# The scheduler's highest rank for the recurrence of a gated DeltaNet layer

## The chip, the cores and the metric

The kernel runs on one core of a Trainium2 chip. The metric is the device time of one execution in microseconds. The core has five engines that work side by side, each through its own queue and in the order of that queue: TensorE (PE in the profile, its weight loads PEld), VectorE (DVE), ScalarE (ACT), GpSimd (POOL) and SyncE (SP), which issues the DMA transfers here.

## The reference

A trunk of two residual layers over 1024 tokens of width 1024, with a last normalization. The even layer has dilated window attention and an HGRN2 recurrence; the change does not touch it. The odd layer is a gated DeltaNet with 8 key heads and 16 value heads of width 128. Its core, cut down:

```python
def odd_mixer(hn, w_in, conv_w, dt_bias, a_log, norm_w, w_out):
    qkv, z, b_logit, a_logit = _split(hn @ w_in, ODD_SIZES)
    qkv = silu(causal_depthwise_conv(qkv, conv_w))
    q, k, v = _split(qkv, (C_KEY_WIDTH, C_KEY_WIDTH, C_VAL_WIDTH))
    ...
    o = gated_delta_rule_chunked(q, k, v, g, beta)
    o = rms_norm(o, norm_w) * silu(z)
    return o @ w_out

def gated_delta_rule_chunked(q, k, v, g, beta):
    # S_t = exp(g_t)(I - b_t k_t k_t^T) S_{t-1} + b_t k_t v_t^T ; o_t = S_t^T q_t
    ...
    sol = triangular_solve(a_mat, rhs, lower=True, unit_diagonal=True)
    u, w = sol[..., :dv], sol[..., dv:]
    def step(state, inp):
        u_n, w_n, a_n, qd_n, kt_n, gl_n = inp
        v_new = u_n - w_n @ state
        o = qd_n @ state + a_n @ v_new
        new_state = state * gl_n + kt_n.T @ v_new
        return new_state, o
```

Every chunk needs the state that the chunk before it left: the step is a chain.

## The kernel before

The 1024 tokens stand as 8 tiles of 128 (NT = 8), and the recurrence goes in 8 chunks of 128 tokens. The odd layer goes through 8 heads `hh`, each one key head with its two value heads (`e` = 0, 1). For each head there are three kinds of work:

- `proj(j)`: the projections by `proj_cols`, in which each product is three matmuls of 128x512 (high and low parts, `mm3`, L143 to L145), for key (pk), two values (pv) and query (pq), each followed by a convolution in `conv` (L822 to L831) on ACT and DVE. `conv` holds a tile `ub`, of which there is one; the projections have two PSUM banks ("pj"). The first thing in `proj(j)` is `way_out(j - 2)`: the normalization of an earlier head's output (POOL, L928), its gate projection (oz), its transposes (ot, L935) and its gating (oy, L937). Weights come by SP (raww) and are split by ACT (w_hi, L112) and DVE (w_lo, L113), one unit ahead of use.
- `invert(hh)`: the inverse of the triangular matrix: products kk (L986), decays gcl (L977, L978), L (L992), copies Lg (L999), then 62 DVE operations, each needing the one before (tm and Tp, L1007 and L1009), then small matmuls (qp, up, q, u).
- `recur(hh)`: the chain. Chunk c: ks = kT·S (L1105); r = ks scaled, plus v (L1108, DVE, two); qs = q·S (L1111); oq = qs scaled (L1114, ACT, two); vp = U·r (L1120); vt = vp scaled (L1123, DVE); vn = copy of vp (L1125, ACT); kv = kn·vt (L1129); S new = S scaled plus kv (L1133, DVE, two); op = A·vn (L1140); then `attend(c + 1)`, which asks for the decays of the chunk after (`decay_a`: a gca load on SP, an addition on POOL at L1079, two exponentials on ACT at L1081) and makes the next chunk's A (qk, L1091, on PE; A, L1093, on DVE); bv = op plus oq (L1143, DVE); oj, squares with their sum (L1148, ACT, two). qs, vp and qk share one PSUM bank ("d"); ks, kv and op share two ("b"); gca and A have two tiles, S two, and r, oq, vt and vn one each.

Three `yield`s cut a chunk into steps. The last loop of the layer emits them mixed with the next head's work: after each step of `recur(hh)`, `mix` emits 2.8 units of `blend(invert(hh + 1), proj(hh + 1))`. For the last head this is the way out of head 6, the gate of head 7 and the first output projections.

What the engines then do is settled when the program is built. A scheduler goes through time by its own model of durations, and on each engine, among the instructions whose inputs and tiles are there, takes the one of lowest rank. An instruction's rank is its place in emission. So in the odd layer the order on every engine, TensorE among them, comes from emission order and the scheduler's model; nothing there is ordered by hand. (The attention of the even layer is emitted in a region that orders TensorE by hand.) On the chip each engine keeps that order and waits on semaphores.

Of the kernel before, what the change touches and what calls it, by code (L numbers as in the profile page):

```python
# [18 lines left out]
P = 128  # L19
D = 1024  # L20
T = 1024
NT = T // P
# [56 lines left out]
def trunk_kernel(ctx: ExitStack, tc: tile.TileContext, x, ew, ewo, ow, owab, owo, nw, fnw, lbl, hnw,  # L79
                 cw, dtb, alog, onw, cst, out):  # L80
    nc = tc.nc
    dve, act, pe, pool = nc.vector, nc.scalar, nc.tensor, nc.gpsimd
# [8 lines left out]
    def bank(tag, shape, name):  # L91
        return pp.tile(shape, F32, name=name, tag=tag, bufs=BANKS[tag])
# [647 lines left out]
    def odd_layer(es):  # L740
        sp = es.enter_context(tc.tile_pool(name="od", bufs=1))
        gt = {n: sp.tile([P, NT, 16], F32, name=f"g_{n}") for n in ("beta", "gc", "ngc", "eg", "nbeg", "etl", "egl")}
# [70 lines left out]
        KT, KN, SC, Q, BV, CQ, SS, VT, US = {}, {}, {}, {}, {}, {}, {}, {}, {}  # L813
# [258 lines left out]
        def recur(hh):  # L1072

            kT, kn, q, bv, U = KT[hh], KN[hh], Q[hh], BV[hh], US[hh]
            ss = SS[hh] = sp.tile([P, NT, 2], F32, name=f"oss{hh}", tag="oss", bufs=2)

            def decay_a(c):
                DA = decays(hh, c, "a")
                pool.tensor_tensor(DA, DA, MA[:, None, :].to_broadcast([P, 2, 128]), op=ALU.add)  # L1079
                for e in range(2):  # L1080
                    act.activation(DA[:, e, :], DA[:, e, :], AF.Exp, bias=gt["ngc"][:, c, 2 * hh + e:2 * hh + e + 1])  # L1081
                return DA

            def attend(c):

                DA = ahead_a.pop()
                if c < NT - 1:
                    ahead_a.append(decay_a(c + 1))
                qk = bank("d", [P, 128], f"qk{hh}_{c}")
                s = slice(c * 128, (c + 1) * 128)  # L1090
                pe.matmul(qk, kT[:, s], q[:, s], start=True, stop=True)  # L1091
                A = sp.tile([P, 2, 128], F32, name=f"A{hh}_{c}", tag="A", bufs=2)
                dve.tensor_tensor(A, qk[:, None, :].to_broadcast([P, 2, 128]), DA, op=ALU.mult)  # L1093
                return A

            ahead_a = [decay_a(0)]
            yield 1.0
            A = attend(0)
            St = None
            for c in range(NT):  # L1100
                col = [slice(2 * hh + e, 2 * hh + e + 1) for e in range(2)]
                s = slice(c * 128, (c + 1) * 128)
                if c:
                    ks = bank("b", [P, 2, 128], f"ks{hh}_{c}")
                    pe.matmul(ks, kT[:, s], St, start=True, stop=True)  # L1105
                    r_ = sp.tile([P, 2, 128], F32, name=f"r{hh}_{c}", tag="r")
                    for e in range(2):
                        dve.scalar_tensor_tensor(r_[:, e, :], ks[:, e, :], SC[hh][:, 1, c, e:e + 1],  # L1108
                                                 bv[:, c, e, :], op0=ALU.mult, op1=ALU.add)
                    qs = bank("d", [P, 2, 128], f"qs{hh}_{c}")  # L1110
                    pe.matmul(qs, q[:, s], St, start=True, stop=True)  # L1111
                    oq = sp.tile([P, 2, 128], F32, name=f"oq{hh}_{c}", tag="oq")
                    for e in range(2):
                        act.activation(oq[:, e, :], qs[:, e, :], AF.Copy, scale=gt["eg"][:, c, col[e]])  # L1114
                else:
                    r_ = bv[:, 0]
                yield 1.0
                vp = bank("d", [P, 2, 128], f"vp{hh}_{c}")
                for e in range(2):
                    pe.matmul(vp[:, e, :], U[:, 2 * c + e, :], r_[:, e, :], start=True, stop=True)  # L1120
                if c < NT - 1:
                    vt = sp.tile([P, 2, 128], F32, name=f"vt{hh}_{c}", tag="vt")
                    dve.tensor_tensor(vt, vp, gt["etl"][:, c, 2 * hh:2 * hh + 2, None].to_broadcast([P, 2, 128]), op=ALU.mult)  # L1123
                vn = sp.tile([P, 2, 128], F32, name=f"vn{hh}_{c}", tag="vn")
                act.copy(vn, vp)  # L1125
                yield 1.0
                if c < NT - 1:
                    kv = bank("b", [P, 2, 128], f"kv{hh}_{c}")
                    pe.matmul(kv, kn[:, c, :], vt, start=True, stop=True)  # L1129
                    Sn = sp.tile([P, 2, 128], F32, name=f"S{hh}_{c}", tag="S", bufs=2)  # L1130
                    if c:
                        for e in range(2):
                            dve.scalar_tensor_tensor(Sn[:, e, :], St[:, e, :], gt["egl"][:, c, col[e]],  # L1133
                                                     kv[:, e, :], op0=ALU.mult, op1=ALU.add)
                    else:
                        dve.tensor_copy(Sn, kv)
                    St = Sn
                op = bank("b", [P, 2, 128], f"op{hh}_{c}")
                for e in range(2):
                    pe.matmul(op[:, e, :], A[:, e, :], vn[:, e, :], start=True, stop=True)  # L1140
                A = attend(c + 1) if c < NT - 1 else None
                if c:
                    dve.tensor_tensor(bv[:, c], op, oq, op=ALU.add)  # L1143
                else:
                    dve.tensor_copy(bv[:, c], op)
                for e in range(2):
                    jk = sp.tile([P, 128], BF16, name=f"oj{hh}_{c}_{e}", tag="jk", bufs=2)
                    act.activation(jk, bv[:, c, e, :], AF.Square, accum_out=ss[:, c, e:e + 1])  # L1148
                yield 1.0


# [41 lines left out]
        for hh in range(8):  # L1193
            fill = proj(hh + 1) if hh < 7 else seq(way_out(6), gate7(), out_last(range(3), ["pj"]))
            if hh < 7:
                fill = blend(invert(hh + 1), fill, 0.8)
            mix(recur(hh), fill, 2.8)
            drain(fill)
# [71 lines left out]
```

## Time and profile before

| what | us |
|---|---|
| median of 3 runs | 2293.18 (2288.69 to 2293.35) |
| the profiled execution | 2290.27 |
| its span | 2288.5 |
| first matmul vp of the first head, from the span's start | 1338.2 |
| last start of an oj of the last head | 2132.1 |

Times within the profile are counted from the start of the span. In a row of the timeline the first number is the start, the second the duration; `op<-vn,A` names what is written and what is read; a bracket holds the time for which the engine stood idle before, and what ended it. TensorE's matmuls overlap: a 128x512 matmul is shown with some 0.39 us, while the next one starts about 0.23 us after it. Each matmul of the recurrence is shown as two instructions, because its operands are plain float32. In the views of waits a PEld row tells of a weight load that stood, a PE row of a matmul.

### The profile page before, as it was taken

How to read it: one execution, taken by the hardware profiler on the slowest of the kernel's cores; microseconds unless marked ns; L12 is line 12 of the kernel's file. 1: busy time of each engine (PE TensorE's matmuls, PEld its weight loads, DVE VectorE, ACT ScalarE, POOL GpSimd, SP SyncE). 2: the span in 40 equal slices, each digit the busy share in tenths (PEclk: the TensorE clock that was granted, in tenths of full speed). 3: DMA queues.
4: the chain of work that ended last, by engine and by line, in shares of the span. 5: the costliest groups of instructions: out<-in, count | busy, mean ns of one | idle time of the engine just before them, and what ended most of it. 6: DMA issues, size and time to landing. Idle time of an engine off the chain costs nothing. (4 is left out here: it accounts for less than half of the span.)

```text
span 2288.5 us, 54642 instructions
## 1 busy us (share of the span) xinstructions
PE 2171.9 (95%) x22597; PEld 1809.0 (79%) x22597; DVE 1427.0 (62%) x3364; ACT 963.4 (42%) x2623; POOL 226.5 (10%) x236
## 2 busy tenths in 40 slices
PE   7999999999999999988999988989899989899998
PEld 6888888898888888866887776767777767678787
DVE  6444444444444444456777887878788877855777
ACT  5333333333333332322236663755555555544223
POOL 0000000000000000000000012131212121210000
PEclk9999999999999999999999998999999999999999
DMA  4111111113222323352323221121212121214232
GB/s 145 38 48 48 44 47 48 43 39 95 78 82 84 90 83 92 97 160 88 102 97 104 59 56 62 53 79 46 76 43 76 52 74 59 65 60 148 91 113 109
DMA packets 101864, 175.83 MB, mean 77 GB/s; under 512 B 16752, under 2 KB 34032, under 8 KB 101616
## 3 DMA queue, kind: packets, MB, share of 16 engines
q1 hardware_dynamic: 101616, 172.35, 24.2%
q8 instruction: 177, 2.90, 0.5%
q14 instruction: 71, 0.58, 0.1%
HBM read 127.07 MB, written 25.23 MB: 67 GB/s over the span
## 5 line engine op out<-in xcount | busy, mean ns | idle before, releaser
L113 DVE TENSOR_TENSOR w_lo<-raww,w_hi 128x512 fp32r<-128x512 f32 x292 | 211.9, 727 | 151.1 <-ACT w_hi L112 147.1
L112 ACT CAST w_hi<-raww 128x512 fp32r<-128x512 f32 x292 | 181.1, 620 | 270.1 <-PE op L145 68.0
L143 PE MATMUL av<-w_hi,hn_hi 128*128 128x256 f32 x512 | 149.0, 291 | 0.0
L143 PE MATMUL bi<-w_hi,hn_hi 128*128 128x256 f32 x512 | 147.0, 287 | 0.0
L144 PE MATMUL bi<-w_lo,hn_hi 128*128 128x256 f32 x512 | 145.3, 284 | 0.0
L144 PE MATMUL av<-w_lo,hn_hi 128*128 128x256 f32 x512 | 144.8, 283 | 0.0
L145 PE MATMUL bi<-w_hi,hn_lo 128*128 128x256 f32 x512 | 144.8, 283 | 0.0
L145 PE MATMUL av<-w_hi,hn_lo 128*128 128x256 f32 x512 | 144.7, 283 | 0.0
L575 ACT ACTIVATE P<-P,nm 128x256 f32<-128x256 f32 (+7 forms) x128 | 71.4, 559 | 130.2 <-DVE nm L573 130.0
L143 PE MATMUL op<-w_hi,yplo 128*128 128x512 f32 x288 | 113.5, 394 | 1.6 <-DVE hr L273 0.9
L145 PE MATMUL op<-w_hi,yplo 128*128 128x512 f32 x288 | 112.2, 390 | 0.0
L144 PE MATMUL op<-w_lo,yplo 128*128 128x512 f32 x288 | 112.1, 389 | 0.0
L143 PE MATMUL pv<-hn_hi,w_hi 128*128 128x512 f32 x256 | 107.0, 418 | 2.6 <-ACT uv L822 2.6
L143 PE MATMUL oz<-hn_hi,w_hi 128*128 128x512 f32 x256 | 109.4, 427 | 0.0
L273 DVE TENSOR_TENSOR hr<-hr,op 128x512 f32<-128x512 f32 x128 | 86.1, 684 | 34.5 <-PE op L145 34.0
L145 PE MATMUL pv<-hn_hi,w_lo 128*128 128x512 f32 x256 | 104.3, 407 | 0.0
L144 PE MATMUL pv<-hn_lo,w_hi 128*128 128x512 f32 x256 | 102.6, 401 | 0.0
L144 PE MATMUL oz<-hn_lo,w_hi 128*128 128x512 f32 x256 | 102.3, 400 | 0.0
L145 PE MATMUL oz<-hn_hi,w_lo 128*128 128x512 f32 x256 | 102.0, 398 | 0.0
L581 DVE STREAM_TRANSPOSE PB<-P 128x256 f32<-128x256 f32 (+3 forms) x64 | 54.6, 854 | 74.9 <-ACT P L575 74.8
L143 PEld LDWEIGHTS av<-w_hi,hn_hi 128*128 128x128 f32 x512 | 97.9, 191 | 3.5 <-issue 1.9
L144 PEld LDWEIGHTS bi<-w_lo,hn_hi 128*128 128x128 f32 x512 | 98.1, 192 | 0.0
(354 smaller groups left out, 6044.9 us busy)
## 6 DMA issues: line engine op xcount, KB each, us to landing
raww<-in_ew_dram SPq DMA_DIRECT2D x128, 256.0 KB, 3.1
raww<-in_ow_dram SPq DMA_DIRECT2D x100, 256.0 KB, 3.0
V<-v SPq DMA_DIRECT2D x256, 64.0 KB, 2.0
rawy<-ymix SPq DMA_DIRECT2D x64, 256.0 KB, 2.7
raww<-in_ewo_dram SPq DMA_DIRECT2D x32, 256.0 KB, 3.0
gcl<-gcd SPq DMA_DIRECT2D x64, 128.0 KB, 3.0
gca<-gcd SPq DMA_DIRECT2D x64, 128.0 KB, 3.0
ymix<-oy SPq DMA_DIRECT2D x32, 256.0 KB, 2.0
```

Of the source, the lines that this page charges most:

```text
L112: act.copy(hi, raw)
L113: dve.tensor_tensor(lo, raw, hi.bitcast(F32), op=ALU.subtract)
L143: pe.matmul(ps, lh, rh, start=start, stop=False)
L144: pe.matmul(ps, lh, rl, start=False, stop=False)
L145: pe.matmul(ps, ll, rh, start=False, stop=stop)
L273: dve.tensor_tensor(dst[:, n], src[:, n], ps, op=ALU.add)
L575: act.activation(Pm[:, e, w0:], Pm[:, e, w0:], AF.Exp, bias=nmx[:, e:e + 1], scale=0.125, accum_out=den[:, i, e:e + 1])
L581: dve.transpose(PB[:, :, i * WG + w0:(i + 1) * WG], Pm[:, :, w0:])
```

## The change

The body of a chunk in `recur` is put under `with tc.high_priority():` in three blocks, one for each step; the `yield`s stay outside. Without an argument this sets the scheduler's rank to 0 (the start of the program) at the beginning of each block and counts up within it; after the block the rank goes on as before. So in each of the three blocks of every chunk and head, ranks begin at 0 again. It holds for all engines, and for what `attend(c + 1)` and `decay_a` emit, as they are called within the third block. `decay_a(0)` and `attend(0)`, before the loop, keep their rank. No instruction, tile or dependency is added or removed, and no region with an order by hand.

```diff
             for c in range(NT):
-                col = [slice(2 * hh + e, 2 * hh + e + 1) for e in range(2)]
-                s = slice(c * 128, (c + 1) * 128)
-                if c:
-                    ks = bank("b", [P, 2, 128], f"ks{hh}_{c}")
-                    pe.matmul(ks, kT[:, s], St, start=True, stop=True)
...
+                with tc.high_priority():
+                    col = [slice(2 * hh + e, 2 * hh + e + 1) for e in range(2)]
+                    s = slice(c * 128, (c + 1) * 128)
+                    if c:
+                        ks = bank("b", [P, 2, 128], f"ks{hh}_{c}")
+                        pe.matmul(ks, kT[:, s], St, start=True, stop=True)
...
                 yield 1.0
-                vp = bank("d", [P, 2, 128], f"vp{hh}_{c}")
...
+                with tc.high_priority():
+                    vp = bank("d", [P, 2, 128], f"vp{hh}_{c}")
                     for e in range(2):
+                        pe.matmul(vp[:, e, :], U[:, 2 * c + e, :], r_[:, e, :], start=True, stop=True)
...
+                    vn = sp.tile([P, 2, 128], F32, name=f"vn{hh}_{c}", tag="vn")
+                    act.copy(vn, vp)
+                yield 1.0
+                with tc.high_priority():
+                    if c < NT - 1:
+                        kv = bank("b", [P, 2, 128], f"kv{hh}_{c}")
+                        pe.matmul(kv, kn[:, c, :], vt, start=True, stop=True)
...
+                    op = bank("b", [P, 2, 128], f"op{hh}_{c}")
                     for e in range(2):
+                        pe.matmul(op[:, e, :], A[:, e, :], vn[:, e, :], start=True, stop=True)
+                    A = attend(c + 1) if c < NT - 1 else None
...
```

More of the change, by code (lines that the diff above doesn't have):

```diff
@@ L1100, in recur @@
             for c in range(NT):
-                col = [slice(2 * hh + e, 2 * hh + e + 1) for e in range(2)]
-                s = slice(c * 128, (c + 1) * 128)
-                if c:
-                    ks = bank("b", [P, 2, 128], f"ks{hh}_{c}")
-                    pe.matmul(ks, kT[:, s], St, start=True, stop=True)
-                    r_ = sp.tile([P, 2, 128], F32, name=f"r{hh}_{c}", tag="r")
-                    for e in range(2):
[L1108 to L1112, printed above, removed]
-                    for e in range(2):
-                        act.activation(oq[:, e, :], qs[:, e, :], AF.Copy, scale=gt["eg"][:, c, col[e]])
-                else:
-                    r_ = bv[:, 0]
@@ L1117, in recur @@
-                yield 1.0
-                vp = bank("d", [P, 2, 128], f"vp{hh}_{c}")
[L1119 to L1130, printed above, removed]
+                with tc.high_priority():
[4 more added lines that the diff above has]
+                        pe.matmul(ks, kT[:, s], St, start=True, stop=True)
+                        r_ = sp.tile([P, 2, 128], F32, name=f"r{hh}_{c}", tag="r")
+                        for e in range(2):
+                            dve.scalar_tensor_tensor(r_[:, e, :], ks[:, e, :], SC[hh][:, 1, c, e:e + 1],
+                                                     bv[:, c, e, :], op0=ALU.mult, op1=ALU.add)
+                        qs = bank("d", [P, 2, 128], f"qs{hh}_{c}")
+                        pe.matmul(qs, q[:, s], St, start=True, stop=True)
+                        oq = sp.tile([P, 2, 128], F32, name=f"oq{hh}_{c}", tag="oq")
+                        for e in range(2):
+                            act.activation(oq[:, e, :], qs[:, e, :], AF.Copy, scale=gt["eg"][:, c, col[e]])
+                    else:
+                        r_ = bv[:, 0]
@@ new lines, in recur @@
+                yield 1.0
+                with tc.high_priority():
+                    if c < NT - 1:
+                        kv = bank("b", [P, 2, 128], f"kv{hh}_{c}")
+                        pe.matmul(kv, kn[:, c, :], vt, start=True, stop=True)
+                        Sn = sp.tile([P, 2, 128], F32, name=f"S{hh}_{c}", tag="S", bufs=2)
+                        if c:
+                            for e in range(2):
+                                dve.scalar_tensor_tensor(Sn[:, e, :], St[:, e, :], gt["egl"][:, c, col[e]],
+                                                         kv[:, e, :], op0=ALU.mult, op1=ALU.add)
+                        else:
+                            dve.tensor_copy(Sn, kv)
+                        St = Sn
+                    op = bank("b", [P, 2, 128], f"op{hh}_{c}")
+                    for e in range(2):
+                        pe.matmul(op[:, e, :], A[:, e, :], vn[:, e, :], start=True, stop=True)
+                    A = attend(c + 1) if c < NT - 1 else None
@@ L1131, in recur @@
                     if c:
-                        for e in range(2):
-                            dve.scalar_tensor_tensor(Sn[:, e, :], St[:, e, :], gt["egl"][:, c, col[e]],
-                                                     kv[:, e, :], op0=ALU.mult, op1=ALU.add)
-                    else:
[L1136 to L1148, printed above, removed]
+                        dve.tensor_tensor(bv[:, c], op, oq, op=ALU.add)
+                    else:
+                        dve.tensor_copy(bv[:, c], op)
@@ L1149, in recur @@
+                    for e in range(2):
+                        jk = sp.tile([P, 128], BF16, name=f"oj{hh}_{c}_{e}", tag="jk", bufs=2)
+                        act.activation(jk, bv[:, c, e, :], AF.Square, accum_out=ss[:, c, e:e + 1])
                 yield 1.0
```

2 lines of the change are left out of this document (added).

## The prediction

> **What bounds the kernel now.** I began with the page, whose engine line names the bound, and then cut the odd layer into stretches with the view of windows (columns: stretch, its length, busy time of PE, PEld, DVE, ACT, POOL, granted clock, DMA share, GB/s).
>
> ```profile
> PE 2171.9 (95%) x22597; PEld 1809.0 (79%) x22597; DVE 1427.0 (62%) x3364; ACT 963.4 (42%) x2623; POOL 226.5 (10%) x236
> ...
> 1336.00:2130.00 794.00, 731.52 (x5046) 590.02 (x5045) 604.47 (x1591) 431.71 (x1293) 150.82 (x166) 0.99 0.22 69
> 1336.00:1400.00 64.00, 54.54 (x307) 43.11 (x305) 52.92 (x159) 36.82 (x116) 9.42 (x12) 0.99 0.22 58
> 1704.00:1811.00 107.00, 99.91 (x701) 81.08 (x700) 85.59 (x225) 61.23 (x183) 21.16 (x23) 1.00 0.20 63
> 2029.00:2130.00 101.00, 97.46 (x478) 80.26 (x478) 53.54 (x120) 41.85 (x126) 14.37 (x15) 1.00 0.37 126
> ```
>
> The reader is to see that TensorE carries the kernel (95%), and that all eight recurrences lie between 1336 and 2130 us. There PE is busy for 731.5 of 794 us, so 62.5 us is all that any reordering can win there: the change removes no matmul. The first recurrence (1336 to 1400) is the poorest stretch, 9.5 us idle in 64. A middle one (1704 to 1811) loses 7.1 in 107, the last one 3.5 in 101. DVE is at 80% in the middle, 53% in the last.
>
> Which waits make the idle time stands in the view of waits, once for the weight loads (PEld, which run ahead and stand first) and once for the matmuls (columns: engine and line, what ended the wait, us in total, times, longest), stretch 1336 to 2132.
>
> ```profile
> PEld op L1140 <- ACT vn L1125: 20.2, 22, 1.9
> PEld vp L1120 <- ACT oq L1114: 13.4, 11, 2.2
> PEld ks L1105 <- issue: 12.7, 10, 2.2
> PEld ot L935 <- POOL bv L928: 8.5, 8, 3.5
> ...
> PEld kv L1129 <- DVE vt L1123: 5.7, 14, 0.8
> PEld vp L1120 <- issue: 5.5, 4, 1.4
> ...
> PE op L1140 <- ACT vn L1125: 12.1, 15, 1.5
> PE vp L1120 <- ACT oq L1114: 8.8, 10, 1.7
> PE ks L1105 <- DVE S L1133: 8.7, 7, 1.8
> ...
> PE vp L1120 <- DVE r L1108: 3.9, 4, 1.0
> ```
>
> The recurrence's own matmuls (ks, vp, kv, op) stand for 20.2 + 13.4 + 12.7 + 5.7 + 5.5 = 57.5 us by the loads and 12.1 + 8.8 + 8.7 + 3.9 = 33.5 us by the matmuls. The matmuls' rows leave out the refilling after a stop, the loads' rows count time in which an earlier matmul still ran; I take the middle, 45 us.
>
> **Why they stand.** The next rows are the timeline of one chunk of the first recurrence.
>
> ```profile
> 1377.82 0.42 DVE L1123 TENSOR_TENSOR vt<-vp,g_etl 128x256 f32<-128x256 f32 x1
> ...
> 1378.05 0.74 POOL L1079 TENSOR_TENSOR gca<-gca,MA 128x256 f32<-128x256 f32 x1 [5.68 <-DVE Tp L1009]
> 1378.15 0.77 DVE L1007 TENSOR_TENSOR tm<-Lp,Tp 128x115 f32<-128x115 f32 x1
> ...
> 1378.82 0.69 ACT L1081 ACTIVATE gca<-gca,g_ngc 128x128 f32<-128x128 f32 x2 [1.74 <-POOL gca L1079]
> ...
> 1379.42 0.35 ACT L1125 COPY vn<-vp 128x256 f32<-128x256 f32 x1
> ...
> 1379.82 0.71 PE L1140 MATMUL op<-vn,A 128*128 128x128 f32 x4 [0.51 <-ACT vn L1125]
> 1379.88 0.27 DVE L1007 TENSOR_TENSOR tm<-Lp,Tp 128x110 f32<-128x110 f32 x1
> ```
>
> vp is free for vn when vt has read it, at 1378.24. But ACT first makes the decay exponentials of a later chunk (gca, emitted earlier, so before it in rank), vn runs at 1379.42, and op, already in TensorE's queue, stands 0.51 us. Every engine issues in order, and the order was fixed at build time by the scheduler's own idea of durations; where a foreign instruction ahead of a step takes longer on the chip, TensorE stands for the difference.
>
> How far the recurrences are stretched shows in the starts of vp, one per chunk: three of the first head, then two neighbours of a middle head.
>
> ```profile
> 1376.90 0.61 PE L1120 MATMUL vp<-r,L 128*128 128x128 f32 x4
> ...
> 1383.77 0.61 PE L1120 MATMUL vp<-r,L 128*128 128x128 f32 x4
> ...
> 1389.85 0.61 PE L1120 MATMUL vp<-r,L 128*128 128x128 f32 x4
> ...
> 1739.28 0.60 PE L1120 MATMUL vp<-r,L 128*128 128x128 f32 x3 [0.47 <-ACT oq L1114]
> 1750.48 0.68 PE L1120 MATMUL vp<-r,L 128*128 128x128 f32 x4 [0.99 <-DVE r L1108]
> ```
>
> The first head goes at 6.1 to 6.9 us a chunk, near the length of its chain; the middle one takes 11.2, since projection work emitted earlier goes first.
>
> **The change part by part.** No instruction is added or removed. What is moved, per chunk: on PE ks, qs, vp, kv, op, qk; on DVE r, vt, S, A, bv; on ACT oq, vn, oj and the gca exponentials; on POOL the gca addition; on SP the gca load. In the three blocks the rank restarts at 0, so each goes ahead of every ready projection, weight-splitting, inversion or gate instruction, and inside the recurrence the chain (ks, kv, vp, r, S, vt at ranks 0 to 2, vn at 3, op at 3 and 4) goes ahead of gca, A and oj.
>
> 1. op behind vn. gca and the inversion's copies no longer stand before vn; at most the one instruction in flight does. Of 20.2 us I keep a quarter, 5. Bounds: 0 and 20.2.
> 2. vp behind oq and r (13.4 + 5.5 = 18.9 us). Same reason, but vp must still wait until both oq have emptied its bank, two ACT steps behind qs. I keep half, 9.5. Bounds: 4 and 30, as now there is often projection work between qs and vp that hides the gap, and at a tighter pace there is less.
> 3. ks behind S and kv behind vt (12.7 + 5.7 = 18.4). The DVE steps pass the substitution but wait for the one in flight. I keep three quarters, 14. Bounds: 9 and 28.
>
> So 57.5 falls to 28.5, half of it; of the 45 us of TensorE time, 22 go.
>
> 4. ot behind POOL's normalization (8.5 us by loads). A recurrence that runs at 6.1 to 6.9 us takes 49 to 55 us of a middle head's 107, so its normalization has some 50 us more before its transposes. I take 4 us gained (bounds 0 and 8.5).
> 5. The last head has little to win (3.5 us idle) and then also runs tight: 2 us lost (bounds 0 and 6).
> 6. Cost for the work that is passed. In the dense 49 to 55 us DVE's demand is near the limit; these are the groups of one middle head (line, tiles, shape, count, busy us, mean ns).
>
> ```profile
> L1007 DVE TENSOR_TENSOR tm<-Lp,Tp 128x126 f32<-128x126 f32 (+22 forms) x31 | 9.4, 303 | 0.7
> L1009 DVE TENSOR_TENSOR Tp<-Tp,tm 128x126 f32<-128x126 f32 (+22 forms) x31 | 8.8, 285 | 0.6
> L113 DVE TENSOR_TENSOR w_lo<-raww,w_hi 128x512 fp32r<-128x512 f32 x12 | 8.3, 688 | 3.9 <-ACT w_hi L112 3.9
> L992 DVE SCALAR_TENSOR_TENSOR L<-kk,sc,gcl 128x128 f32<-128x128 f32 x16 | 4.9, 345 | 3.6 <-ACT gcl L978 3.5
> L1108 DVE SCALAR_TENSOR_TENSOR r<-ks,sc,bv 128x128 f32<-128x128 f32 x15 | 4.7, 343 | 0.3 <-PE ks L1105 0.3
> L827 DVE SCALAR_TENSOR_TENSOR kT<-uk,cws,kT 128x512 f32<-128x512 f32 x6 | 4.7, 786 | 0.1
> L1133 DVE SCALAR_TENSOR_TENSOR S<-S,g_egl,kv 128x128 f32<-128x128 f32 x12 | 4.0, 339 | 0.4 <-PE kv L1129 0.4
> L1093 DVE TENSOR_TENSOR A<-qk,gca 128x256 f32<-128x256 f32 x8 | 3.3, 418 | 0.7 <-PE qk L1091 0.7
> L1123 DVE TENSOR_TENSOR vt<-vp,g_etl 128x256 f32<-128x256 f32 x7 | 2.9, 420 | 0.9 <-PE vp L1120 0.7
> L1143 DVE TENSOR_TENSOR bv<-op,oq 128x256 f32<-128x256 f32 x7 | 2.9, 416 | 0.0
> ```
>
> The recurrence takes 4.7 + 4.0 + 3.3 + 2.9 + 2.9 = 17.8 us of DVE, the substitution 18.2, L 4.9, half of the weight splitting 4.2: 45 us in 49 to 55. What is passed waits, and convolutions hold the single buffer ub meanwhile, so two banks of projection later TensorE would stand. Nearest row: the first recurrence at this pace shows no such wait of a projection, so I take 1 us a head for heads 1 to 6, 6 us (bounds 0 and 40).
>
> The sum is -22 - 4 + 2 + 6 = **-18 us**. SP and POOL cost nothing in it. On SP's queue the gca load passes weight loads; one decay is asked for a chunk ahead, about 6 us at this pace, and 3.0 us for the load, 0.74 on POOL and 0.69 on ACT (above) make 4.4. If that cover of 1.6 us goes, A is late, A keeps bank d, and qs and vp stand behind it: up to 1 us a chunk, which is inside bounds 2. Weight loads that are passed wait for one transfer of 128 KB and are asked for a unit ahead. On POOL the gca addition passes normalization and gating, which nothing in the dense part waits for.
>
> ```profile
> gca<-gcd SPq DMA_DIRECT2D x64, 128.0 KB, 3.0
> ```
>
> The profiled execution took 2290.27 us (span 2288.5 and 1.8 us around it), 2.9 below the median of 2293.18. From it, 2290.3 - 18 = **2272 us**.
>
> A rule against the change: the Trainium skill (SBUF — State Buffer, "SBUF: two separate sides") says that VectorE with two SBUF inputs and GpSimd take a shared pair of ports by turns, each for a whole instruction. The trace agrees: tm at 1378.15 took 0.77 us beside POOL's gca, 0.27 at 1379.88 without. By that rule the eight gca additions, now packed into the dense part, would each cost the substitution about 0.5 us there, 4 us a head, and the sum would be nearer to the slower case below.
>
> **The rivals.** (a) No change (chance 0.16): the waits only change their place. TensorE still has every matmul, the tighter pace takes away the projection work that now lies between steps, and what is won at op comes back at vp and ks: 2290 us, within 0.2%, which is about what a measurement of this kernel can tell. That the rank does nothing belongs here: if the chain and not the rank sets the pace, vp stays at 11 us. Against it speaks that the first head shows 6.1.
> (b) Slower (0.27): VectorE becomes the bound of the dense part. The groups above with the key convolution (4.7) and all of the weight splitting (8.3) ask for 17.8 + 18.2 + 4.9 + 4.7 + 8.3 = 53.9 us. It decides where this exceeds the recurrence's length, 49 us at 6.1 a chunk: then the convolution waits, keeps ub, and TensorE stands for up to 4.9 us a head, 34 us over seven heads. With the gains of steps 1 to 4 still made, the time is 2290 - 24 + 34 = 2300 us; with none of them 2324; I put it between, at 2312. For it speaks the first head, at this pace TensorE's poorest stretch (15% idle); against it, what that stretch waits for (the same view of loads, 1336 to 1400), since most of it should go:
>
> ```profile
> PEld op L1140 <- ACT vn L1125: 6.4, 6, 1.9
> PEld ot L935 <- POOL bv L928: 4.3, 2, 3.5
> ```
>
> (c) Much faster (0.10): all 45 us and ot's go, and earlier release of buffers helps the inversion: 2240 us.
>
> **How the numbers follow.** Forecast 0.47 at 2272 (own range 2254 to 2285), (a) 0.16, (b) 0.27, (c) 0.10. Faster by over 0.2%: 0.47 + 0.10 = 0.57; within: 0.16; slower: 0.27. The range leaves out half of (c) and the upper half of (b): 2243 to 2316.
>
> **What would show it.** Right: vp starts 5.5 to 7 us apart in the middle heads; op behind vn falls from 20.2 to about 5 us; PE's idle time between 1336 and the last oj falls from 62.5 to about 45 us; tm and Tp stretch out past the recurrence. Wrong: a projection's matmul (pk, pv) among the waits with more than a few us, or vp behind oq above 19 us: then (b) or (a). If vp still starts 11 us apart, the rank did nothing.

## The result and the profile after

The changed kernel took 2309.86 us (median of 4 runs, 2305.26 to 2315.41), the kernel before 2292.9 beside it: ratio 1.0079, 95% interval 1.0054 to 1.0104. It is **slower by 17 us**, where 2272 was forecast. The time lies inside the range and near the price of rival (b), but by another way.

The profiled execution took 2305.26 us (span 2303.5). First the engine line of its page, then the view of windows (columns as before): all eight recurrences, then a middle head.

```profile
PE 2188.1 (95%) x22597; PEld 1809.6 (79%) x22597; DVE 1441.2 (63%) x3364; ACT 964.9 (42%) x2623; POOL 221.3 (10%) x236
```

```profile
1336.00:2145.00 809.00, 749.15 (x5050) 592.91 (x5049) 617.68 (x1599) 432.91 (x1295) 152.22 (x172) 0.98 0.23 67
1714.00:1824.00 110.00, 102.84 (x704) 82.27 (x703) 87.89 (x226) 61.55 (x182) 20.08 (x23) 0.98 0.21 61
```

The same matmuls keep PE busy for 16 us longer (2188.1 against 2171.9), while its idle time in the eight recurrences hardly falls (62.5 us before, 809.00 - 749.15 = 59.9 now). Part of this is a slower PE: the granted clock is 0.98 in the whole stretch, where it was 0.99. DVE is at 80% in the middle head, as before.

The rank itself took hold. In the timeline two neighbouring vp of a middle head, first rows, start 5.5 us apart; before it was 11.2. All eight heads now show 4.9 to 7.2.

```profile
1738.02 0.69 PE L1122 MATMUL vp<-r,L 128*128 128x128 f32 x4
...
1743.53 0.71 PE L1122 MATMUL vp<-r,L 128*128 128x128 f32 x4 [0.36 <-ACT oq L1115]
```

So the chain runs at the pace that was expected, and the time grows. Where TensorE then stands is in the view of waits, loads first, stretch 1300 to 2180 (lines have moved by 1 to 3: op is L1143, vn L1127, vp L1122, oq L1115, kv L1132, vt L1125).

```profile
PEld op L1143 <- ACT vn L1127: 28.4, 41, 1.6
PEld vp L1122 <- ACT oq L1115: 24.8, 46, 2.3
PEld qp L1030 <- DVE Un L1013: 18.0, 7, 3.3
PEld kv L1132 <- DVE vt L1125: 15.8, 40, 1.5
PEld ot L935 <- POOL bv L928: 6.9, 6, 2.1
...
PEld ks L1106 <- PE qk L1091: 1.3, 6, 0.4
```

```profile
PE qp L1030 <- DVE Un L1013: 15.1, 7, 2.9
PE op L1143 <- ACT vn L1127: 14.8, 19, 1.2
PE vp L1122 <- ACT oq L1115: 10.0, 12, 1.9
```

ks no longer waits for S. But op behind vn, which should have fallen to 5, rose from 20.2 to 28.4, kv behind vt from 5.7 to 15.8, and there is a new lump: qp, the first matmul behind the substitution, stands 2.1 to 2.9 us in each of six heads, and 0.4 in a seventh. No projection (pk, pv) is among the waits.

**Why op stands.** The timeline of one chunk (head 4), shortened to the rows that matter:

```profile
1756.10 0.42 DVE L1125 TENSOR_TENSOR vt<-vp,g_etl 128x256 f32<-128x256 f32 x1 [1.00 <-PE vp L1122]
...
1756.80 0.72 POOL L1079 TENSOR_TENSOR gca<-gca,MA 128x256 f32<-128x256 f32 x1 [6.04 <-DMA gca<-gcd]
...
1757.56 0.40 ACT L1081 ACTIVATE gca<-gca,g_ngc 128x128 f32<-128x128 f32 x1 [1.04 <-POOL gca L1079]
1757.87 0.35 ACT L1127 COPY vn<-vp 128x256 f32<-128x256 f32 x1
...
1758.27 0.71 PE L1143 MATMUL op<-vn,A 128*128 128x128 f32 x4 [0.99 <-ACT vn L1127]
...
1765.90 0.41 DVE L1093 TENSOR_TENSOR A<-qk,gca 128x256 f32<-128x256 f32 x1
```

vn could have run when vt had read vp, at 1756.52. ScalarE, idle for 1.04 us, held it back behind an exponential, which waited for GpSimd's addition, which waited for its load. op stood 0.99 us. Counted in pairs from the first, this exponential belongs not to the next chunk's decay but to the one after: vn is of chunk 4, the exponential of chunk 6, whose A reads it only at 1765.90 (last row). It was not late for its own use; it stood ahead of vn with more than 7 us to spare.

Booked over the layer, op lost about 22 us, 21 times, behind a vn that stood behind such a waiting pair of exponentials. In the kernel before it was about 10 us, 10 times, and the prediction's own row at 1378.82 is one of them: ScalarE stood idle for 1.74 us ahead of that pair, while vn could have run from 1378.24. (A pair counts as waiting here when ScalarE stood idle ahead of either of its two exponentials beyond the time at which vn could have run. Some expectations below go by the second exponential alone and so call the pairs of the kernel before running; the first of each had waited.) So the wait is old, and the change has made it more frequent: an exponential stands right ahead of 26 of the 64 vn, of 15 in the kernel before.

**The lump at qp**, the same timeline, PE alone:

```profile
1790.61 0.39 PE L143 MATMUL pv<-hn_hi,w_hi 128*128 128x512 f32 x1
1790.83 0.39 PE L144 MATMUL pv<-hn_lo,w_hi 128*128 128x512 f32 x1
1793.49 1.25 PE L1030 MATMUL qp<-Un,L 32*32 32x32 f32 x64 [2.27 <-DVE Un L1013]
1794.67 0.80 PE L145 MATMUL pv<-hn_hi,w_lo 128*128 128x512 f32 x1
1795.27 0.63 PE L143 MATMUL pv<-hn_hi,w_hi 128*128 128x512 f32 x1
1795.69 0.63 PE L144 MATMUL pv<-hn_lo,w_hi 128*128 128x512 f32 x1
1796.12 0.63 PE L145 MATMUL pv<-hn_hi,w_lo 128*128 128x512 f32 x1
```

The substitution, which the recurrence now passes on DVE, ends later than the order allowed for. After the wait the large matmuls start 0.43 us apart, before it 0.22.

**A tally.** Waits overlap with work, so I also booked TensorE's lost time by itself: for each two neighbouring matmuls of the trace, the distance of their starts less that of an undisturbed pair of the kind (0.229 us behind a 128x512, 0.2165 behind ks, qs or kv, 0.112 behind vp, op or qk), put to the later one, and what falls into half clock put there. Five kernels (e3, e5, e11: below), us from 1215 us to the end:

```
              before   after      e5      e3     e11
ks, qs          17.9     7.2    11.2     7.5     7.7
vp              17.7    19.7    14.7    18.4    14.2
kv               3.8    10.5     6.9     8.1     4.2
op              17.3    26.5     8.9    11.4     5.2
qp               0.9    15.7    18.9     9.4    10.2
other inversion 21.6    11.9     9.7    18.4    17.8
ot, tk, tq, tv  16.8    23.3    21.8    30.8    23.7
half clock      10.5    16.9    19.2    12.1    10.1
rest            16.7     6.0    11.1    19.6    21.6
sum            123.3   137.7   122.3   135.7   114.6
span          2288.5  2303.5  2288.2  2301.2  2280.5
```

The sums differ as the spans do (after less before: 14.4 and 15.0), so the table is complete (the rest holds the projections' own small gaps, and is too low where a small matmul hides in the next one). The change wins 10.7 us at ks and qs and 9.7 within the inversion, and loses 9.2 at op, 6.7 at kv, 2.0 at vp, 14.8 at qp, 6.5 at the transposes and 6.4 to the clock; the rest, which I can't resolve, is 10.7 us better.

### The profile page after: what moved, and what is told of

Read it like the earlier page. It is cut to its first block, busy times and chain, and to the rows that moved or that the text cites. A ratio compares the mean times of both kernels' runs of the same rounds, so it can differ in the third digit from the quotient of the medians.

```text
span 2303.5 us, 54709 instructions
## 1 busy us (share of the span) xinstructions
PE 2188.1 (95%) x22597; PEld 1809.6 (79%) x22597; DVE 1441.2 (63%) x3364; ACT 964.9 (42%) x2623; POOL 221.3 (10%) x236
## 5 line engine op out<-in xcount | busy, mean ns | idle before, releaser
L145 PE MATMUL oz<-hn_hi,w_lo 128*128 128x512 f32 x256 | 109.1, 426 | 0.0
L144 PE MATMUL oz<-hn_lo,w_hi 128*128 128x512 f32 x256 | 107.6, 420 | 0.0
L145 PEld LDWEIGHTS av<-w_hi,hn_lo 128*128 128x128 f32 x512 | 97.9, 191 | 0.4 <-issue 0.4
```

The costliest lines, as they stand in the source:

```text
L144: pe.matmul(ps, lh, rl, start=False, stop=False)
L145: pe.matmul(ps, ll, rh, start=False, stop=stop)
```

## The experiments

Four theories were tried. **L**: the loss is the inversion's lag, paid at qp and by the clock after it. **G**: it is vn behind exponentials that wait for GpSimd's late addition. **D**: it is VectorE's part of the chain passing other work. **P** against **S**: the effects belong to the rank and the exponentials' place, or to the luck of one order. The expectations name their rivals R, C, A and B and say what each means. Ratios are to the kernel before, run on the same chip.

| run | edit | median us | ratio, 95% interval |
|---|---|---|---|
| e1 | changed, qp emitted later | 2312.99 | 1.0101 (1.0078 to 1.0123) |
| e2 | changed, TensorE kept awake | 2311.28 | 1.0089 (1.0072 to 1.0105) |
| e3 | rank on all engines but TensorE | 2306.15 | 1.0059 (1.0042 to 1.0076) |
| e4 | rank on TensorE alone | 2306.92 | 1.0065 (1.0050 to 1.0081) |
| e5 | changed, exponentials behind vn | 2291.03 | 1.0010 (0.9999 to 1.0021) |
| e6 | rank for oq, vn alone | 2299.31 | 1.0042 (1.0028 to 1.0056) |
| e7 | rank for r, vt, S alone | 2293.05 | 1.0018 (1.0006 to 1.0030) |
| e8 | e6, exponentials behind vn | 2280.13 | 0.9958 (0.9946 to 0.9971) |
| e9 | before, exponentials behind vn | 2282.58 | 0.9953 (0.9937 to 0.9969) |
| e10 | changed, decays two chunks ahead | 2321.28 | 1.0127 (1.0111 to 1.0142) |
| e11 | e3, exponentials behind vn | 2276.66 | 0.9933 (0.9917 to 0.9949) |
| e12 | e6 and e7, exponentials behind vn | 2282.11 | 0.9953 (0.9939 to 0.9968) |
| e13 | changed, additions two chunks ahead | 2311.07 | 1.0086 (1.0072 to 1.0100) |
| e14 | e3, additions two chunks ahead | 2306.45 | 1.0078 (1.0064 to 1.0091) |
| e15 | changed, longer yield behind qp | 2311.07 | 1.0080 (1.0063 to 1.0097) |
| e16 | e5, longer yield behind qp | 2292.09 | 1.0001 (0.9992 to 1.0010) |
| e17 | e3, longer yield behind qp | 2301.78 | 1.0041 (1.0027 to 1.0055) |
| e18 | e11, longer yield behind qp | 2275.99 | 0.9936 (0.9922 to 0.9950) |

**The lump and the clock: e1, e2.** e1 puts thirty units of filler ahead of qp in the emission; e2 adds five tiny matmuls a head that read the substitution's intermediate Tp, so that its lag is paid in small parts.

```diff
# e1, ahead of the bank of qp
+            yield 30.0, 0.0
# e2, in the substitution's loop
+                if k in (12, 18, 22, 26, 29):
+                    if k == 12:
+                        qp = bank("c", [P, 16, 32], f"qp{hh}")
+                    pe.matmul(qp[0:16, 0, 0:16], Tp[:, k + 1, :], Tp[:, k + 1, :], start=True, stop=True)
```

> The changed kernel with one line more: before the first small matmuls of the inversion (qp) a yield of 30 units, so that they are emitted later; in heads 4 to 7 they stand 9, 46, 46 and 43 projection matmuls later in TensorE's queue, in heads 0 to 3 where they stood. Theory L (VectorE's lag behind the scheduler's plan is paid in one lump at qp, 15.1 us in seven waits, and each lump of 2 to 3 us is followed by 3 to 10 us at half the TensorE clock): the waits of qp for Un in heads 4 to 7 go, some 8 us, and with them 3 stretches of 3 us at half clock, 4 us: about 12 us below the changed kernel, 2298. Theory R (the recurrence's own waits at its tight pace, and projections that wait for a passed convolution, cost the 17 us): nothing of these is touched, within 4 us of the changed kernel.

> The changed kernel with five tiny added matmuls a head that read the substitution's tile after steps 12, 18, 22, 26 and 29 and write into qp's bank, which qp overwrites. TensorE so meets VectorE five times on the way to qp. Theory L: the sum of waits for the substitution stays near 15 us, but in pieces below 1 us; stretches at half clock after qp (some 28 us in the profile of the changed kernel) go, and the time falls by 6 to 12 us, to about 2300, less some 3 us that the added matmuls cost. If the clock has no part in the loss, the time stays or grows by up to 5 us. Theory R: no gain, 2310 to 2315.

Neither gave time back. In e1 the wait of qp went as meant, but the transposes took its place (waits of PE, 1300 to 2180):

```profile
PE tk L840 <- DVE kT L831: 9.6, 6, 2.0
...
PE tv L890 <- DVE vT L831: 7.2, 6, 2.4
PE up L1038 <- DVE Q L1033: 6.9, 4, 4.1
...
PE qp L1031 <- DVE Un L1013: 3.9, 3, 2.0
```

e2's mean clock rose to 0.991 (0.987 in the changed kernel, 0.993 before), and the time stayed at 2311: the lag of VectorE's work is paid somewhere, in one lump or in twelve waits. The lower clock follows from the lump, and mending it gave no time back; what it is worth alone is not separated, since e2 also adds 40 matmuls and moves the waits.

**Which engine's rank: e3, e4, e6, e7.** Each puts `with tc.high_priority():` around some statements of the recurrence alone.

```diff
# e4: the same around qk, ks, qs, vp, kv, op and around nothing else
+                    with tc.high_priority():
                         pe.matmul(ks, kT[:, s], St, start=True, stop=True)
# e6: around the two lines on ScalarE that the chain needs
+                        with tc.high_priority():
                             act.activation(oq[:, e, :], qs[:, e, :], AF.Copy, scale=gt["eg"][:, c, col[e]])
...
+                with tc.high_priority():
                     act.copy(vn, vp)
```

> The kernel before with rank 0 for the recurrence's DVE, ACT, POOL and SP instructions alone; its matmuls keep the rank of emission. Theory L: the recurrence keeps the pace of the matmuls' emission, so it still meets the substitution on VectorE, and no lump of more than 1.5 us stands at qp; op's wait behind vn falls. Between 2280 and 2295, near the kernel before. Theory R: passing other work on DVE and ACT is what costs, so most of the 17 us comes: 2303 or more.

> The kernel before with rank 0 for the recurrence's matmuls alone; DVE, ACT, POOL and SP keep the rank of emission. Theory L: chunks come closer than in the kernel before but DVE still follows emission; the lump at qp depends on whether a recurrence still runs beside the substitution, and as its DVE steps wait behind older work it does: 2288 to 2298. Theory R: the tight order on TensorE is what costs (op, vp and kv stand at steps that are late): 2303 or more.

> The kernel before with rank 0 for oq and vn alone, the chain's two ACT steps; DVE, POOL, SP and TensorE keep emission order. Theory G and D (rank on DVE makes the inversion and the convolutions late, rank on TensorE puts op and kv at the planned instant; ACT is half idle and has nothing to pay): waits of op and vp fall by some 8 us, nothing else moves: 2280 to 2288. Rival C: within 4 us of the kernel before.

> The kernel before with rank 0 for r, vt and S alone, the chain's DVE steps. Theory D (what is passed on DVE is paid at qp, tk, tv and ot: plus 19 us with rank on all engines but TensorE): ks loses some 8 us less, but qp, tk, tv and ot together 10 to 20 us more: 2294 to 2304. Rival (the loss of the variant with rank off TensorE came from POOL's and SP's gca or from ACT): 2285 to 2291.

e3 and e4 came out as theory R has it: the two halves cost about as much each as the whole (13 to 15 us against 17), so they don't add up. e6 and e7 came out in neither of their ranges. TensorE's rank without the vector engines' makes the matmuls arrive early and stand: in e4 op behind vn is the largest wait of PE, 19.5 us.

```profile
PE op L1146 <- ACT vn L1129: 19.5, 22, 2.0
PE vp L1124 <- ACT oq L1117: 11.0, 10, 2.3
PE kv L1134 <- DVE vt L1127: 7.7, 9, 1.3
```

The rank for VectorE's chain alone (e7) costs 4 us (1 to 7 by its interval), less than D has. The one for oq and vn alone (e6) should have shortened exactly the waits for ScalarE, and cost 10 us; op behind vn stayed (12.0 us by PE, 12.1 before), because the exponentials, though not ranked, still stood ahead of vn.

**The exponentials behind vn: e5, e8, e9, e11, e12.** `tc.issue_after` fixes the order of issue when the program is built. `decay_a` keeps the load and the addition where they were; its two exponentials are emitted by their own function in `attend(c + 1)`, in an order that puts them behind vn of chunk c on ScalarE. They are so asked for one chunk later than before, and just ahead of the A that reads them. No semaphore is added, since both are on one engine.

```diff
-                for e in range(2):
-                    act.activation(DA[:, e, :], DA[:, e, :], AF.Exp, bias=gt["ngc"][:, c, 2 * hh + e:2 * hh + e + 1])
                 return DA
+            def expo(DA, c, vn_):
+                with tc.issue_after(vn_.ins) if vn_ is not None else ExitStack():
+                    for e in range(2):
+                        act.activation(DA[:, e, :], DA[:, e, :], AF.Exp, bias=gt["ngc"][:, c, 2 * hh + e:2 * hh + e + 1])
```

> The changed kernel, with the two decay exponentials (gca) on ACT tied behind vn of the chunk before; the gca load and POOL's addition stay where they were. Theory G (op stands since vn is queued on ACT behind gca, which stands for POOL's late addition: 19 us of the 26 us that op loses in the changed kernel): op's loss falls to below 8 us, the time by 12 to 19 us, to 2291 to 2298. Rival C (the losses are conserved: what is not paid at op is paid at the next step of the same chain, kv or vp): op's loss falls, kv and vp rise by as much, 2305 to 2312.

> The kernel before with rank 0 for oq and vn and with the gca exponentials tied behind vn of the chunk before. Theory G: op's loss goes below 5 us from 17; 2275 to 2285, below the kernel before by 6 to 16 us. Rival C: within 4 us of the kernel before.

> The kernel before with one edit: the two exponentials of chunk c+1's decay are issued behind vn of chunk c; no rank is changed. Theory G (what costs is a vn queued on ScalarE behind exponentials that still wait for GpSimd's addition; that becomes frequent only with the rank): in the kernel before, vn stood 9.7 us behind exponentials that were running and none behind ones that waited, so the tie alone brings at most those, 2281 to 2291. Rival A (the tie is a gain by itself, whatever the rank, and the 19 us between e6 and e8 come from it): 2268 to 2280.

> The rank for the recurrence on VectorE, ScalarE, GpSimd and SyncE but not TensorE (as in e3) and the exponentials behind vn. e3 had little of this loss (4.4 us behind exponentials, against 19 us in the changed kernel) and was 2306 by dearer transposes and by the lump at qp. Theory G: a gain of at most 8 us over e3, 2296 to 2306. Rival A (the tie is worth its 19 us in every version): 2282 to 2292.

> Rank for six statements alone, oq and vn on ScalarE and r, vt and both forms of S on VectorE, and the exponentials behind vn (e8 with VectorE's part of the chain). e8 gave 2280; its ks still waited 11.4 us for S and its vp 5.6 us for r. If those waits go and nothing takes their place: 2262 to 2275. Rival D (the work that VectorE's chain passes, the inversion above all, comes late, as qp did in the changed kernel): 2278 to 2292, with the wait of qp or kk up by as much as ks and vp lose.

e5 gives 19 us back, all that the change had cost. Its waits (loads, then PE) show where:

```profile
PEld vp L1126 <- ACT oq L1119: 19.1, 46, 1.6
PEld qp L1030 <- DVE Un L1013: 17.1, 6, 3.9
PEld op L1147 <- ACT vn L1131: 12.2, 33, 1.1
PEld kv L1136 <- DVE vt L1129: 10.4, 29, 1.5
```

```profile
PE op L1147 <- ACT vn L1131: 2.3, 6, 0.7
```

op fell from 28.4 to 12.2 by the loads and from 14.8 to 2.3 by PE; in the tally from 26.5 to 8.9, with kv and vp 8.6 better besides. qp's lump is still there, and the clock is no better: they are not what e5 mended. In its timeline the addition returns no earlier; vn no longer cares:

```profile
1729.31 0.37 ACT L1131 COPY vn<-vp 128x256 f32<-128x256 f32 x1
1729.58 0.69 ACT L1085 ACTIVATE gca<-gca,g_ngc 128x128 f32<-128x128 f32 x2
1729.67 0.73 POOL L1079 TENSOR_TENSOR gca<-gca,MA 128x256 f32<-128x256 f32 x1 [3.57 <-DMA gca<-gcd]
...
1729.87 0.61 PE L1147 MATMUL op<-vn,A 128*128 128x128 f32 x4
```

The tie is worth something in every version: 11 us in the kernel before (e9), 19 from e6 to e8, 29 from e3 to e11, where G allowed 8 and A said 19: both missed. The mean time from the first matmul of vp to vn, over all chunks, follows it: 2.58 to 2.27 us (before to e9), 1.75 to 1.45 (changed to e5), 2.13 to 1.90 (e3 to e11), 2.54 to 2.16 (e6 to e8). Sixty-four chunks by 0.23 to 0.38 us are 15 to 24 us. Of the 128 exponentials, the number that was one of the two instructions before a vn fell from 37 to 6, 30 to 9, 34 to 4 and 28 to 6. Between e3 and e11 the tie does more than that: 19 exponentials were among the two instructions before an oq in e3, 2 in e11, and the time from the start of qs to the end of the second oq fell from 2.12 to 1.65 us. How much of the 29 us comes by oq is not separated; in the changed kernel it was 2 exponentials, in e5 1.

e12 came out in D's range: adding VectorE's part to e8 gains nothing. In the tally ks loses 10 us less, while vp, qs, op, qp, q and u together lose some 15 more.

**Late addition, or the place alone: e10, e13, e14.** If the exponentials cost only because the addition is late, an earlier load should do what the tie does. A third buffer for gca pays for that; vt shares r's buffer.

```diff
# e10: load, addition and exponentials two chunks ahead
-                DA = ahead_a.pop()
-                if c < NT - 1:
-                    ahead_a.append(decay_a(c + 1))
+                DA = ahead_a.pop(0)
+                if c < NT - 2:
+                    ahead_a.append(decay_a(c + 2))
# e13, e14: load and addition two chunks ahead, exponentials one
+                DA = ready_a.pop()
+                if c < NT - 1:
+                    expo(c + 1)
+                if c < NT - 2:
+                    ahead_a.append(decay_a(c + 2))
```

> The changed kernel with the decay's load, GpSimd addition and exponentials asked for two chunks ahead in place of one (a third buffer; vt shares a buffer with r, which costs no wait, since r of the next chunk waits for kv anyhow). Nothing is tied. Theory G (vn waits because the exponentials ahead of it wait for a late addition): with a chunk more of lead the addition is done, the 19 us of op behind such exponentials fall under 5, and the time is 2287 to 2298. Rival B (it is the exponentials' own time on ScalarE between vp and vn, about 0.3 us each, whenever they stand there): op's loss stays at 15 to 27 us and the time at 2303 to 2315.

> The changed kernel with the decay's load and GpSimd's addition two chunks ahead (a third buffer, vt sharing with r as in e10), the exponentials one chunk ahead as they were; nothing is tied. Theory G: the exponentials find their addition done, so a vn behind them waits for their running time at most; the 19 us of op behind exponentials that waited fall under 4, those behind running ones stay under 10, and the time is 2287 to 2300. Rival B (the exponentials' own time between vp and vn): op's loss stays over 20 us, the time at 2303 to 2318.

> The same edit in the kernel of e3 (rank on every engine but TensorE). Theory G: as the tie did in e11, 2273 to 2290. Rival (e11's 29 us under e3 are an order that the tie happened to give, not the wait that it took away): 2295 to 2312.

All three missed G's numbers. e13 came out in B's range and e14 in its rival's; e10 was slower than either had it. But they don't decide between G and B, since ScalarE's waits for the addition hardly fell. The rows are e10's and e13's (61.7 us, 53 times, in the changed kernel):

```profile
ACT gca L1081 <- POOL gca L1079: 60.6, 51, 2.9
```

```profile
ACT gca L1085 <- POOL gca L1079: 53.6, 45, 3.0
```

In e10 each load is still issued when an A frees a buffer, and comes back in the same phase of a chunk, 3 us later, as its timeline shows:

```profile
1748.56 0.42 DVE L1093 TENSOR_TENSOR A<-qk,gca 128x256 f32<-128x256 f32 x1
1749.00 0.32 SPq L963 DMA_DIRECT2D gca<-gcd  x1
...
1751.98 0.73 POOL L1079 TENSOR_TENSOR gca<-gca,MA 128x256 f32<-128x256 f32 x1 [19.70 <-DMA gca<-gcd]
```

In e13 the exponentials are only asked for later. With the third buffer they became ready earlier, and they moved up on ScalarE with the addition: an exponential three chunks on stands ahead of 28 of the 64 vn, in the changed kernel of none. So they still followed their addition at once and waited for it. Booked as above, op's loss behind waiting pairs is about 23 us in e10 and 17 in e13 (22 in the changed kernel), and about 4 in e14 (5 in e3). The 11 us by which e10 is slower still were not traced.

So **G's place is shown, and its reason is not separated from the place**. The tie takes away both at once: ScalarE's waits for the addition fall from 65.9 to 8.2 us between the kernel before and e9, and from 87.4 to 2.8 between e3 and e11. Op's loss behind exponentials that only ran is 0.5 to 2.4 us in the kernel before, the changed one, e3, e10, e13 and e14, so nearly all of it lies behind ones that waited. A version in which the exponentials keep their place and none waits was not made.

**Tie or luck: e15 to e18.** The scheduler's order changes with any edit, so the four versions that carry the argument were run again with a longer yield behind qp, which was meant to shuffle the order and to do nothing else.

```diff
# behind qp, in invert
-            yield 1.5, 1.3
+            yield 2.0, 1.3
```

> The changed kernel with the neutral edit alone. Theory P (the place of the exponentials ahead of vn, and the inversion's lag paid at qp, belong to the rank in any order): 2300 to 2318, the wait of qp over 10 us, op behind vn over 12. Rival S (the loss is the luck of one order): under 2298.

> e5 with the neutral edit. Theory P: 12 to 24 us under e15. Rival S: less than 8 us under it, or above it.

> e3 with the neutral edit. Theory P: 2298 to 2312. Rival S: under 2295.

> e11 with the neutral edit. Theory P: 18 us or more under e17, and at least 8 under e16, since TensorE's rank costs the lump at qp. Rival S: within 10 us of e17 or of e16.

All four came out in P's ranges, but two of them test nothing. In e15 and e16 the edit left the order as it was: by tile and shape, ScalarE's sequence in their traces is that of the changed kernel and of e5, and TensorE's 22,597 instructions differ by one or two swapped neighbours. They are repeats (2311.07 beside 2309.86 us, 2292.09 beside 2291.03). In e17 and e18 the order did move, by some 260 and 290 lines of such a comparison on TensorE and 110 to 120 on ScalarE.

So without TensorE's rank the tie gives 25.8 us in one order and 29.5 in another, and e17 is again slower than the kernel before (9 us; e3 14). With the rank on every engine only one order with the tie was run. For the loss itself there are more: e1, e2, e10 and e13 each have an order of their own, and all took 2311 to 2321 us. TensorE's rank costs 14.4 us with the tie from e11 to e5, and 16.1 from e18 to e16. The waits of e18 show what is left (loads):

```profile
PEld vp L1129 <- ACT oq L1123: 12.8, 18, 2.2
PEld qp L1030 <- DVE Un L1013: 10.8, 5, 4.1
PEld ot L935 <- POOL bv L928: 9.2, 11, 2.0
PEld up L1037 <- DVE Q L1032: 9.0, 6, 2.1
```

Between e16 and e18 qp loses 9.5 us less in the tally, the half clock 8.7 and op 6.2. The version of e11 and e18, rank on every engine but TensorE and the exponentials behind vn, **beats both kernels**: 2276 us, 0.7% under the kernel before. Most of that is the tie's: e9, the tie without any rank, is 0.5% under it, and the intervals of e9 and e11 overlap.

What stays open: of the 21 us between the sums of e3 and e11, op, kv and vp make 14.3 and the transposes 7.1; why the transposes gain by the tie was not traced.

## Why the prediction was wrong

- **Step 1, op behind vn, is the step that failed.** It said that gca no longer stands before vn, because inside the recurrence the chain "goes ahead of gca, A and oj". It rests on a misreading of the kernel before: the exponentials at 1378.82 were not "emitted earlier". They make the decay of chunk 7, which `attend(6)` asks for in the third step of chunk 5, behind vn of chunk 5 in the second. They had the later rank already, and stood first all the same. A rank only chooses among what is ready by the scheduler's model; the exponentials were ready while vn still waited for vp, so they took the free place on ScalarE, and on the chip they held vn back. Putting the chain at rank 0 could not change that. 28.4 us stood where 5 were forecast, and with the exponentials tied behind vn (e5) the whole 17 us are gone.
- **That is not the whole distance to the forecast.** e5 mends step 1 and still ends at 2291 us, some 19 above 2272. The other part is step 6.
- **The cover of 1.6 us** on the gca load, priced at nothing with up to 1 us a chunk in bounds 2, did not break. The load is issued as soon as an A frees a buffer, earlier than the sum had it, and A never waits for an exponential in the views of the changed kernel. I had looked for damage by lateness, at A, qs and vp. The damage came at vn, by exponentials that ScalarE has ahead of it long before A needs them.
- **Step 2** (vp behind oq and r, 18.9 to 9.5): 24.8, within its bounds, on the wrong side. The prediction's own sign of being wrong, vp behind oq above 19, came true.
- **Step 3** (ks and kv, 18.4 to 14): 15.8 + 1.3 = 17.1. ks went almost wholly and kv took its place.
- **Step 4** (ot, -4): 8.5 to 6.9, a gain of 1.6 by the loads, hardly any in the tally. **Step 5**: the end of the layer gained instead of losing 2. The out-projection's matmuls begin at 2116.7 in place of 2093.3 and the rest then takes 186.8 us in place of 195.2, 8 us less; I put it down to the way out, more of which was done before, but that was not traced.
- **Step 6** (6 us for the work that is passed) is the term that was priced too low, and at the wrong place. No projection waited for a convolution; the substitution came late, and qp paid 14.8 us with 6.4 of half clock behind it, 21 us where 6 were forecast. Part of this was won back within the inversion (9.7). Its nearest row, the first recurrence "at this pace", was not at that pace throughout: two of its seven steps from vp to vp take 8.7 and 10.8 us.
- **The rule of the shared ports** holds for the single instruction and is small in the sum. In the timeline of the changed kernel tm took 1.33 us beside one of GpSimd's operations:

```profile
1780.88 1.29 POOL L937 TENSOR_TENSOR oy<-oy,g 128x512 f32<-128x512 f32 x1 [4.47 <-ACT oy L936]
...
1780.99 1.33 DVE L1007 TENSOR_TENSOR tm<-Lp,Tp 128x126 f32<-128x126 f32 x1
```

  But all tm from 1300 to 2180 us, by groups of instructions (before, then after), grew by 3.2 us, not by 4 a head:

```profile
L1007 DVE TENSOR_TENSOR tm<-Lp,Tp 128x126 f32<-128x126 f32 (+22 forms) x236 | 71.4, 303 | 3.7
```

```profile
L1007 DVE TENSOR_TENSOR tm<-Lp,Tp 128x126 f32<-128x126 f32 (+22 forms) x236 | 74.6, 316 | 4.5
```

- **Rival (b)** had the right sign, and its price (2312) was right by luck: its mechanism didn't occur. VectorE is not the bound of the dense part. In the view of windows, the recurrence of the middle head (first row) has DVE busy for 35.0 of 47 us, 74%, since half of the substitution and most of the weight splitting come later. It is busy for 94% only behind the recurrence (second row), where the rest of the substitution runs toward qp at 1793.49.

```profile
1732.00:1779.00 47.00, 42.69 (x227) 33.33 (x226) 34.95 (x102) 33.67 (x110) 9.68 (x11) 1.00 0.26 75
1779.00:1795.00 16.00, 13.73 (x123) 11.28 (x122) 15.11 (x46) 7.25 (x25) 3.87 (x5) 0.98 0.22 71
```

  Two sums of the rivals are slightly off: the 24 us "of steps 1 to 4" in (b) include step 5 (without it they are 26), and the 45 + 8.5 us of (c) give 2237, not 2240.
- **Rival (a)** had the better sentence, that the waits only change their place. I counted the pace of the chain as the gain. With the tie in both, the rank without TensorE is worth at most some 5 us, which the intervals don't tell from nothing (e9 to e11), and the rank with TensorE costs 8 us (e9 to e5; 13 by their ratios).

## What to carry to other kernels

A rank for a scheduler is no order: work with slack that becomes ready first still takes the place ahead of the chain on an engine that issues in order. Look, for each step of a chain, at the instruction right ahead of it on its engine; if it belongs to something that may come later, tie it behind the step before ranking anything. And a tighter chain is a gain only where TensorE stood for it. Ranking TensorE too cost 14 to 16 us here, most of it at qp and by the half clock behind it; that the work which used to cover the inversion was then used up is my reading, which no run tested.

## What the runs showed of the hardware

- **Half clock after short waits.** Waits of 2.1 to 2.9 us at qp in six heads of the changed kernel were followed by stretches of 3.4 to 10.2 us in which the large matmuls start 0.43 us apart in place of 0.22 (rows above). The Trainium skill (TensorE: Matmul & The Clock Gate, "What's actually happening") puts the drop behind an idle window of about 3.4 us. In the rows above, 2.27 us of wait and 1.2 us of 32x32 matmuls came together before it; whether the small matmuls count as idle, no run here separates.
- **A better clock, and no time.** e2 raised the mean clock from 0.987 to 0.991, and the time did not follow.
